# Forgetting attention: the product of weights and values with the values stationary and split in two parts

## The chip, the cores and the metric

The kernel runs on one core of one Trainium2 chip. The metric is device time in microseconds (us); lower is better. TensorE (PE) multiplies matrices: it holds a stationary operand, moves a second one past it, and writes sums to PSUM. VectorE (DVE), ScalarE (ACT) and GpSimd (POOL) work elementwise; SyncE (SP) issues the transfers. Each engine takes its instructions in a fixed order.

## The reference, cut to what matters

The program is a chain of two transformer blocks on 1024 tokens of width 1024. The change lies in the second block, in one of its three mixers, an attention with 8 heads of width 64 over 1040 tokens (16 meta tokens and 1024 others), causal, with a forgetting bias `c` (a running sum of log-sigmoids):

```python
s = jnp.einsum('bhqd,bhkd->bhqk', qb, kh).astype(jnp.float32) + (cb[..., :, None] - c[..., None, :])
s = jnp.where(kpos[None, :] <= qpos[:, None], s, -jnp.inf)
p = jax.nn.softmax(s, axis=-1)
return jnp.einsum('bhqk,bhkd->bhqd', p.astype(vh.dtype), vh)
```

Beside it run a recurrent mixer (RWKV, in chunks of 128 tokens) and a gated linear recurrence. Their outputs go through an output projection and then a feed-forward network with a gate.

## The kernel before, in words

One program holds all stages; a scheduler in the language orders the instructions of each engine at build time by a simulated timeline, with what is written first taken first. So parts that don't depend on each other are interleaved: `block2` (L1536) writes RWKV's chunks (L1553), then the projections of the attention (`fox_proj`, L1555), then `fox_att` (L1565); on the chip the attention fills the gaps of RWKV's last chunks, whose last operation on the output rows is L1302.

`fox_att` (L1442) loops over 8 heads. For each it loads the raw queries and keys (`fraw`, L1464, SyncE's queue) and splits each into a high part rounded to the type fp32r and a low rest (L1471 to L1477: ScalarE, VectorE, GpSimd; the query's and key's rows 64 to 127 carry rests and the bias). For an even head it loads the values of two heads (L1479 to L1481). Query tiles are 9: one of 16 rows, eight of 128 (`TILES`, L1364). `pipe` (L551) keeps two generators going, so that the first half of one tile's work is written next to the second half of the one before.

`fox_tile` (L1489) does one query tile `i`. First half: per chunk of up to 512 keys two fp32r products and a mask product into PSUM (L1506 to L1509), evacuation with a row maximum on VectorE (`evac_max`, L397), the negated maximum (L1514 to L1517), the exponential with its row sum on ScalarE (L1519), and the reciprocal (L1521). Second half: `wT` (L399) turns the weights, one transpose for each key tile (L405), with one copy from PSUM by ScalarE for up to four of them (L407); then, for each key tile, a plain fp32 product with the turned weights stationary and 64 columns of values moving (L1531), which the profile shows as two records; then the scaling by the reciprocal (L1532). In the odd head of a pair the tile's output rows are stored (L1534, SyncE's queue).

After the last head `done` frees RWKV's memory and loads the output weights, cast by ScalarE (L103) with the rest on VectorE (L106) in `wout_load` (L685). `out_proj2` (L1568) follows, one 128-row tile after another.

Of the PSUM banks (512 columns each) the attention uses two for scores (`sc`), two for transposes (`te`), one for the sums of the value products (`po`).

## Time and profile before

| | |
|---|---|
| Median of 3 runs | 3175.73 us (3175.03 to 3179.65) |
| Profiled execution, its own time | 3179.39 us |
| Span of the profile | 3177.6 us, 52057 instructions |
| TensorE busy | 3058.7 us (96%) |
| TensorE weight load busy | 2780.7 us (88%) |
| VectorE busy | 1863.2 us (59%) |
| ScalarE busy | 1401.9 us (44%) |
| GpSimd busy | 467.1 us (15%) |

The span runs from the first to the last instruction of the profiled execution. A busy TensorE is modelled, as its instructions overlap: the distance between starts says more than a duration. PEclk is the granted clock as a share of 2.4 GHz; the two levels are 1.2 and 2.4 GHz, so 0.59 means mostly the lower one. A row with a count covers that many instructions. "[1.86 <-DVE fo L1532]" behind a row is idle time of the engine before it and what ended it. The attention's first head starts at 2035 us of the span and the last one ends at 2305 us.

### The profile page before, as it was taken

Reading aid. Unit: us, or ns where it says so; the run is one execution under the profiler, and the core shown is the slowest. Engines: PE = TensorE matmul, PEld = TensorE weight load, DVE = VectorE, ACT = ScalarE, POOL = GpSimd, SP = SyncE. Lnnn points to the kernel's source line nnn. Section 1 sums busy time; section 2 is a strip of 40 time slices with the busy share of each in tenths; the row PEclk is TensorE's granted clock in tenths of the full one; section 3 lists DMA queues with packets and bytes.
Section 4 is the critical chain, followed back from the end, with each engine's and each line's share of the span. In section 5 each row is a group of like instructions: output and inputs, shape, how many; then the busy total and the mean of one; then the engine's idle time right before and its main releaser. Section 6 shows DMA issues by size and latency. Waiting matters only on the chain.

```text
span 3177.6 us, 52057 instructions
## 1 busy us (share of the span) xinstructions
PE 3058.7 (96%) x19891; PEld 2780.7 (88%) x19891; DVE 1863.2 (59%) x4889; ACT 1401.9 (44%) x3415; POOL 467.1 (15%) x506
## 2 busy tenths in 40 slices
PE   8899999999999999998999999999999999999997
PEld 5799999889878789997889999788879999999996
DVE  5777757677766665446547434666555344454446
ACT  4679845555553643323236121445534433233323
POOL 2467622331220000000000000201000000000003
PEclk9999999999999999999999899898999999999999
DMA  5222210110043221113321121313132111111113
GB/s 212 71 74 89 85 40 6 32 33 7 15 138 107 100 101 57 57 39 101 126 67 49 58 69 46 90 41 97 34 123 94 49 40 47 47 47 57 44 41 116
DMA packets 140330, 218.22 MB, mean 69 GB/s; under 512 B 24408, under 2 KB 80784, under 8 KB 140080
## 3 DMA queue, kind: packets, MB, share of 16 engines
q1 hardware_dynamic: 140080, 214.90, 21.5%
q8 instruction: 156, 2.56, 0.3%
q14 instruction: 94, 0.77, 0.1%
HBM read 171.87 MB, written 42.97 MB: 68 GB/s over the span
## 4 chain that ended last, share of the span: by engine, by line
PE 80%; DVE 7%; ACT 5%; DMA 3%; issue 2%; POOL 1%; SPq 0%; DVEq 0%; POOLq 0%; ACTq 0%
PE mm L132 17%; PE mm L133 16%; PE mm L134 16%; PE po L1531 3%; PE te L405 3%; PE sc L134 2%; PE sc L132 2%; PE sc L133 2%; PE sc L391 2%; PE po L661 2%; PE po L611 1%; DMA woraw<-in_w_out 1%; ACT EB L646 1%; ACT EA L596 1%; PE mm L149 1%
## 5 line engine op out<-in xcount | busy, mean ns | idle before, releaser
L132 PE MATMUL mm<-whi,hT 128*128 128x256 f32 (+1 forms) x1760 | 513.4, 292 | 15.3 <-DVE gs L428 3.4
L133 PE MATMUL mm<-wlo,hT 128*128 128x256 f32 (+1 forms) x1760 | 508.3, 289 | 3.9 <-POOL wlo L106 3.8
L132 PEld LDWEIGHTS mm<-whi,hT 128*128 128x128 f32 x1760 | 337.6, 192 | 24.1 <-ACT v L549 4.6
L133 PEld LDWEIGHTS mm<-wlo,hT 128*128 128x128 f32 x1760 | 337.7, 192 | 8.0 <-POOL wlo L106 5.1
L132 PE MATMUL mm<-hT3h,whi 128*128 128x342 f32 (+3 forms) x1020 | 325.9, 320 | 0.0
L133 PE MATMUL mm<-hT3l,whi 128*128 128x342 f32 (+3 forms) x1020 | 325.2, 319 | 0.0
L134 PE MATMUL mm<-hT3h,wlo 128*128 128x342 f32 (+3 forms) x1020 | 324.7, 318 | 0.0
L134 PE MATMUL mm<-whi,lo 128*128 128x256 f32 x1040 | 300.0, 289 | 2.5 <-POOL lo L106 2.4
L103 ACT CAST whi<-wraw 128x512 fp32r<-128x512 f32 (+2 forms) x205 | 136.0, 678 | 211.2 <-PE mm L133 85.0
L132 PE MATMUL mm<-hT,whi 128*128 128x352 f32 (+3 forms) x640 | 219.8, 344 | 2.9 <-ACT a L1018 1.8
L1659 DVE TENSOR_TENSOR acc<-acc,sc 128x512 f32<-128x512 f32 x160 | 108.8, 686 | 193.6 <-PE sc L134 192.8
L407 ACT COPY wT<-te 128x512 f32<-128x512 f32 (+2 forms) x368 | 160.5, 454 | 136.3 <-PE te L405 133.5
L133 PE MATMUL mm<-hT,whi 128*128 128x352 f32 (+3 forms) x640 | 218.7, 342 | 0.1
L134 PE MATMUL mm<-hT,wlo 128*128 128x352 f32 (+3 forms) x640 | 218.5, 343 | 0.0
L106 DVE TENSOR_TENSOR wlo<-wraw,whi 128x512 fp32r<-128x512 f32 (+1 forms) x161 | 126.0, 790 | 152.2 <-ACT whi L103 151.5
L134 PE MATMUL mm<-whi,hT 128*128 128x256 f32 (+3 forms) x720 | 205.8, 286 | 0.0
L134 PEld LDWEIGHTS mm<-whi,lo 128*128 128x128 f32 x1040 | 201.0, 193 | 5.2 <-POOL lo L106 3.3
L133 PEld LDWEIGHTS mm<-hT3l,whi 128*128 128x128 f32 x1020 | 192.0, 188 | 6.3
L132 PEld LDWEIGHTS mm<-hT3h,whi 128*128 128x128 f32 x1020 | 191.8, 188 | 6.0
L134 PEld LDWEIGHTS mm<-hT3h,wlo 128*128 128x128 f32 x1020 | 191.9, 188 | 3.6
L97 POOL TENSOR_TENSOR inv<-inv,cm 128x1 f32<-128x1 f32 (+1 forms) x87 | 53.2, 611 | 889.1 <-DVE inv L95 889.1
L97 POOL TENSOR_TENSOR c<-c,cm 128x2 f32<-128x2 f32 (+1 forms) x170 | 124.4, 733 | 384.5 <-DVE c L95 346.0
(491 smaller groups left out, 7740.8 us busy)
## 6 DMA issues: line engine op xcount, KB each, us to landing
adraw<-in_adaln_w SPq DMA_DIRECT2D x48, 512.0 KB, 3.8
wraw<-in_ffn_up SPq DMA_DIRECT2D x85, 256.0 KB, 2.8
wraw<-in_w_ab SPq DMA_DIRECT2D x26, 512.0 KB, 3.9
woraw<-in_w_out SPq DMA_DIRECT2D x48, 256.0 KB, 3.0
wraw<-in_w_gla SPq DMA_DIRECT2D x48, 256.0 KB, 2.8
wraw<-in_w_in SPq DMA_DIRECT2D x24, 512.0 KB, 4.3
dnraw<-in_ffn_down SPq DMA_DIRECT2D x44, 256.0 KB, 2.6
fraw<-qkd SPq DMA_DIRECT2D x32, 260.0 KB, 4.1
```

Source lines behind the costliest of these rows:

```text
L97: nc.gpsimd.tensor_tensor(out, out, self.cm05[:p, :n], op=ALU.pow)
L103: nc.scalar.copy(hi, src)
L106: (lo_eng or nc.vector).tensor_tensor(lo, src, hi.bitcast(F32), op=ALU.subtract)
L132: mmul(ps, ah, bh, start=k == 0, stop=False)
L133: mmul(ps, ah, bl, start=False, stop=False)
L134: mmul(ps, al, bh, start=False, stop=k == nk - 1)
L391: self.nc.tensor.matmul(sp, q[x][:, m], keys, start=x == 0, stop=last and x == 1)
L405: nc.tensor.transpose(ps[:n, j * 128:j * 128 + nq], E, self.ident[:nq, :nq])
L407: nc.scalar.copy(w[:n, :m, :nq], ps.rearrange("p (j t) -> p j t", j=4)[:n, :m, :nq])
L661: nc.tensor.matmul(ops[:, :128], w[:, x, :], v[:, i], start=x0 + x == 0, stop=x0 + x == len(kt) - 1)
L1531: nc.tensor.matmul(ops[:n, :64], w[:kn, y, :n], v[:kn, x, r], start=x == 0, stop=x == i)
L1659: nc.vector.tensor_tensor(acc[:, t, sl], acc[:, t, sl], ps, op=ALU.add)
```

## The change

Values become the stationary operand. For each head the values are split into an fp32r high part and a low rest that lie side by side (`vs`, 128 columns). Query tiles are handled in three groups, (0 to 3), (4 to 6) and (7, 8), by the new function `fox_tiles`. For each key tile `x` the weights of all query tiles of the group that see it are turned into one bank (up to 400 columns), copied to SBUF by ScalarE, rounded to fp32r (`hi`: ScalarE for even `x`, GpSimd for odd), and the rest taken by GpSimd (`lo`); two fp32r products, `hi` and `lo`, move past the same stationary values and add up over key tiles in one bank. The sums then lie with 64 + 64 value rows on partitions and query rows on columns; they are copied, turned back by one transpose for each query tile, and the two halves added and scaled. The evacuation of scores takes the negated scores and their minimum, which saves the separate negation. Buffers for a prepared head go from three to two, the value buffer from two to one, and the exponentials' buffers from four of one tile to two of one group. The output rows are stored at the end of a group. Where the removed lines only repeat the function printed above they are cut.

```diff
--- before.py
+++ after.py
@@ -1447,7 +1447,7 @@
         s0 = p.tile([128, 8], F32, name="foxsel0", bufs=1)
         nc.sync.dma_start(s0, I["fox_sel"])
         nc.vector.tensor_copy(sel, s0)
-        kcs = [p.tile([128, T], F32R, name=f"fkc{i}", bufs=1) for i in range(3)]
+        kcs = [p.tile([128, T], F32R, name=f"fkc{i}", bufs=1) for i in range(2)]
         cn = p.tile([128, T], F32, tag="fraw", name="cn")
         nc.sync.dma_start(cn[64:128], cnd)
         for kc in kcs:
@@ -1464,10 +1464,10 @@
                         nc.sync.dma_start(raw[64 * e:64 * e + 64], qkd[pr, part, r])
                     raws.append(raw)
 
-                qh = p.tile([128, T], F32R, tag="fqh", name="fqh", bufs=3)
-                ql = p.tile([128, T], F32R, tag="fql", name="fql", bufs=3)
-                kh = p.tile([128, T], F32R, tag="fkh", name="fkh", bufs=3)
-                kc = kcs[h % 3]
+                qh = p.tile([128, T], F32R, tag="fqh", name="fqh")
+                ql = p.tile([128, T], F32R, tag="fql", name="fql")
+                kh = p.tile([128, T], F32R, tag="fkh", name="fkh")
+                kc = kcs[h % 2]
                 nc.scalar.activation(qh, raws[0], AF.Copy, scale=0.125)
                 nc.vector.scalar_tensor_tensor(ql[0:64], raws[0][0:64], 0.125, qh[0:64].bitcast(F32), op0=ALU.mult,
                                                op1=ALU.subtract)
@@ -1476,62 +1476,100 @@
                 nc.gpsimd.tensor_copy(kc[0:64], kh[0:64])
                 nc.vector.tensor_tensor(kh[64:128], raws[1][64:128], kh[64:128].bitcast(F32), op=ALU.subtract)
                 if m == 0:
-                    v = p.tile([128, 9, 128], F32, tag="fv", name="fv")
+                    v = p.tile([128, 9, 128], F32, tag="fv", name="fv", bufs=1)
                     nc.sync.dma_start(v[:16, 0], vd[0:16, pr * 128:pr * 128 + 128])
                     nc.sync.dma_start(v[:, 1:9], vd[16:1040, pr * 128:pr * 128 + 128].rearrange("(t p) d -> p t d", p=128))
                     o = p.tile([128, 9, 128], F32, tag="fo", name="fo", bufs=1)
-                for i in range(9):
-                    yield self.fox_tile(pr, m, i, qh, ql, kh, kc, v, o, o2d)
+
+                vs = p.tile([128, 9, 2, 64], F32R, tag="fvs", name="fvs")
+                for z in ((slice(0, 128), slice(1, 9)), (slice(0, 16), slice(0, 1))):
+                    nc.scalar.copy(vs[z][:, :, 0], v[z][:, :, r])
+                    nc.gpsimd.tensor_tensor(vs[z][:, :, 1], v[z][:, :, r], vs[z][:, :, 0].bitcast(F32), op=ALU.subtract)
+                for tiles in ((0, 1, 2, 3), (4, 5, 6), (7, 8)):
+                    yield self.fox_tiles(pr, m, tiles, qh, ql, kh, kc, vs, o, o2d)
             done()
 
         self.pipe(heads())
 
-    def fox_tile(self, pr, m, i, qh, ql, kh, kc, v, o, o2d):
+    def fox_tiles(self, pr, m, tiles, qh, ql, kh, kc, vs, o, o2d):
 
         nc, p = self.nc, self.ap_
-        T = 1040
         r = slice(64 * m, 64 * m + 64)
-        c0, n = self.TILES[i]
-        nk = c0 + n
-        if i == 0:
-            cks = [(0, 16)]
-        else:
-            cks = [(0, min(nk, 400))] + [(a, min(512, nk - a)) for a in range(400, nk, 512)]
...
+        ends = [c0 + n for c0, n in self.TILES]
+        E_ = p.tile([128, 1968], F32, tag="fE", name="fE")
+        l, nM = self.small(4, "fl"), self.small(4, "fnM")
+        Es, cols, a, c = [], [], 0, 0
+        for y, i in enumerate(tiles):
+            c0, n = self.TILES[i]
+            nk = ends[i]
+            E = E_[:, a:a + nk]
+            Es.append(E)
+            cols.append(slice(c, c + n))
+            a, c = a + nk, c + n
+            cks = [(0, min(nk, 400))] + [(x, min(512, nk - x)) for x in range(400, nk, 512)]
+
+            mx = nM[:, y:y + 1] if len(cks) == 1 else self.small(4, "fmx")
+            for ci, (k0, kn) in enumerate(cks):
+                sp = self.sc()
+                ks = slice(k0, k0 + kn)
+                last = ci == len(cks) - 1
+                nc.tensor.matmul(sp[:n, :kn], qh[:, c0:c0 + n], kh[:, ks], start=True, stop=False)
+                nc.tensor.matmul(sp[:n, :kn], ql[:, c0:c0 + n], kc[:, ks], start=False, stop=not last)
+                if last:
+                    nc.tensor.matmul(sp[:n, kn - n:kn], self.ident_r[:n, :n], self.masks_r[:n, 2, :n],
+                                     start=False, stop=True)
+                nc.vector.tensor_scalar(E[:n, ks], sp[:n, :kn], -1.0, None, op0=ALU.mult, op1=ALU.min,
+                                        accum_out=mx[:n, ci:ci + 1])
+            if len(cks) > 1:
+                nc.vector.tensor_reduce(nM[:n, y:y + 1], mx[:n, :len(cks)], axis=AX.X, op=ALU.min)
+            nc.scalar.activation(E[:n], E[:n], AF.Exp, bias=nM[:n, y:y + 1], scale=-1.0, accum_out=l[:n, y:y + 1])
+        rl = self.small(4, "frl")
+        small = 1 if tiles[0] == 0 else 0
+        if small:
+            nc.vector.reciprocal(rl[:16, :1], l[:16, :1])
+        nc.vector.reciprocal(rl[:, small:len(tiles)], l[:, small:len(tiles)])
         yield
+
         ops = self.po()
-        steps = [(self.wT([E[:n, 0:16]], n), 0, 0)]
-        for x0 in range(1, i + 1, 4):
-            grp = range(x0, min(x0 + 4, i + 1))
-            w = self.wT([E[:n, self.TILES[x][0]:self.TILES[x][0] + 128] for x in grp], n)
-            steps += [(w, y, x) for y, x in enumerate(grp)]
-        for w, y, x in steps:
-            kn = self.TILES[x][1]
-            nc.tensor.matmul(ops[:n, :64], w[:kn, y, :n], v[:kn, x, r], start=x == 0, stop=x == i)
-        nc.vector.tensor_scalar(o[:n, i, r], ops[:n, :64], rl[:n], None, op0=ALU.mult)
+        for x in range(tiles[-1] + 1):
+            ys = [y for y, i in enumerate(tiles) if i >= x]
+            k0, kn = self.TILES[x]
+            ps = self.te()
+            for y in ys:
+                n = cols[y].stop - cols[y].start
+                nc.tensor.transpose(ps[:kn, cols[y]], Es[y][:n, k0:k0 + kn], self.ident[:n, :n])
+            z = slice(0, kn), slice(cols[ys[0]].start, c)
+            et = p.tile([128, 400], F32, tag="fet", name="fet")
+            nc.scalar.copy(et[z], ps[z])
+            hi = p.tile([128, 400], F32R, tag="feh", name="feh")
+            lo = p.tile([128, 400], F32R, tag="fel", name="fel")
+            if x % 2:
+                nc.gpsimd.tensor_copy(hi[z], et[z])
+            else:
+                nc.scalar.copy(hi[z], et[z])
+            nc.gpsimd.tensor_tensor(lo[z], et[z], hi[z].bitcast(F32), op=ALU.subtract)
+            w = vs[:kn, x].rearrange("p e d -> p (e d)")
+            for e, h in enumerate((hi, lo)):
+                nc.tensor.matmul(ops[:, z[1]], w, h[z], start=x + e == 0, stop=e == 1 and x == tiles[-1],
+                                 skip_group_check=True)
+        ot = p.tile([128, 400], F32, tag="fot", name="fot")
+        nc.scalar.copy(ot[:, :c], ops[:, :c])
+        ps = self.te().rearrange("p (y e d) -> p y e d", y=4, e=2)
+        for y in range(len(tiles)):
+            n = cols[y].stop - cols[y].start
+            nc.tensor.transpose(ps[:n, y].rearrange("p e d -> p (e d)"), ot[:, cols[y]], self.ident)
+        t = p.tile([128, 4, 64], F32, tag="ft", name="ft")
+        parts = [(slice(0, 128), slice(small, len(tiles)))] + [(slice(0, 16), slice(0, 1))] * small
+        for rows, ys in parts:
+            nc.scalar.copy(t[rows, ys], ps[rows, ys, 1])
+            nc.vector.tensor_tensor(t[rows, ys], t[rows, ys], ps[rows, ys, 0], op=ALU.add)
+            shape = [rows.stop, ys.stop - ys.start, 64]
+            nc.vector.tensor_tensor(o[rows, tiles[0] + ys.start:tiles[0] + ys.stop, r], t[rows, ys],
+                                    rl[rows, ys].unsqueeze(2).to_broadcast(shape), op=ALU.mult)
         if m == 1:
-            nc.sync.dma_start(o2d[i][:, pr * 128:pr * 128 + 128], o[:n, i])
+            for i in tiles:
+                n = self.TILES[i][1]
+                nc.sync.dma_start(o2d[i][:, pr * 128:pr * 128 + 128], o[:n, i])
 
     def block2(self, close_hT, w2, first, o2d, lod):
```

## Rows read from the trace of the kernel before

**Rows 1.** Windows: length, busy (xcount) of PE, PEld, DVE, ACT, POOL; granted clock, DMA share, GB/s.

```profile
2035.00:2182.00 147.00, 146.76 (x1099) 127.79 (x1097) 105.99 (x400) 72.41 (x181) 17.77 (x19) 1.00 0.18 44
2182.00:2200.00 18.00, 16.14 (x77) 14.88 (x76) 8.43 (x25) 8.28 (x22) 1.74 (x1) 0.59 0.74 198
2236.00:2306.00 70.00, 69.53 (x523) 60.79 (x523) 34.67 (x174) 40.74 (x113) 0.00 (x0) 1.00 0.08 22
```

**Rows 2.** PE's timeline: head starts 0, 3, 5, 7, and the last value products; start, length.

```profile
2035.13 0.39 PE L405 MATMUL te<-ident_r,fE 16*16 16x16 f32 x2
2166.36 0.18 PE L405 MATMUL te<-ident_r,fE 16*16 16x16 f32 x1
2235.51 0.18 PE L405 MATMUL te<-ident_r,fE 16*16 16x16 f32 x1
2281.97 0.18 PE L405 MATMUL te<-ident_r,fE 16*16 16x16 f32 x1
2304.22 1.10 PE L1531 MATMUL po<-fv,wT 128*128 128x64 f32 x8
```

**Rows 3.** PE's timeline in head 7: start, length, instruction, count.

```profile
2299.36 1.58 PE L1531 MATMUL po<-fv,wT 16*128 16x64 f32 x10
2300.78 0.27 PE L405 MATMUL te<-ident_r,fE 128*16 128x128 f32 x1
2300.88 0.78 PE L1531 MATMUL po<-fv,wT 128*128 128x64 f32 x6
2301.50 1.04 PE L405 MATMUL te<-ident_r,fE 128*128 128x128 f32 x8
2302.47 1.47 PE L1531 MATMUL po<-fv,wT 16*128 16x64 f32 x10
```

**Rows 4.** Chain of waits between 2182 and 2236 us: start, length, what.

```profile
2183.32 1.98 DVE fkh L1477
2221.60 3.04 DMA woraw<-in_w_out
```

**Rows 5.** PE's timeline in head 6: two score pairs, 400 and 512 columns.

```profile
2266.22 0.43 PE L1506 MATMUL sc<-fkh,fqh 128*128 128x400 f32 x1
2266.48 0.34 PE L1507 MATMUL sc<-fkc,fql 128*128 128x400 f32 x1
2266.66 0.39 PE L1506 MATMUL sc<-fkh,fqh 128*128 128x512 f32 x1
2266.89 0.39 PE L1507 MATMUL sc<-fkc,fql 128*128 128x512 f32 x1
```

**Rows 6.** Groups of instructions, 2020 to 2306 us, ScalarE: count, busy us, mean ns, idle before.

```profile
L407 ACT COPY wT<-te 128x512 f32<-128x512 f32 x48 | 27.6, 583 | 28.5 <-PE te L405 28.1 <-PE po L1531 0.3
L407 ACT COPY wT<-te 128x256 f32<-128x256 f32 x16 | 5.9, 369 | 6.5 <-PE te L405 6.5
L103 ACT CAST wo<-woraw 128x512 fp32r<-128x512 f32 x16 | 9.8, 612 | 7.9 <-DMA woraw<-in_w_out 7.9
L1475 ACT CAST fkh<-fraw 128x1040 fp32r<-128x1040 f32 x8 | 8.4, 1052 | 10.1 <-DMA fraw<-qkd 9.9
```

**Rows 7.** Groups of instructions: GpSimd in the whole run, VectorE in 2020 to 2306 us.

```profile
L182 POOL TENSOR_TENSOR adacc<-adacc,adpr 128x512 f32<-128x512 f32 x84 | 108.7, 1296 | 40.2 <-ACT adpr L179 27.3 <-ACT adacc L179 7.3 <-PE sc L391 3.2
L182 POOL TENSOR_TENSOR adacc<-adacc,adpr 128x256 f32<-128x256 f32 x28 | 20.7, 739 | 13.8 <-ACT adpr L179 6.6 <-ACT adacc L179 5.8
L1474 POOL CAST fql<-foxsel 64x1040 fp32r<-64x1040 f32 x8 | 8.6, 1081 | 63.7 <-PE sc L1507 52.6 <-PE sc L1509 9.7 <-DVE foxsel L1449 1.3
...
L106 DVE TENSOR_TENSOR wo<-woraw,wo 128x512 fp32r<-128x512 f32 x16 | 11.5, 717 | 9.2 <-ACT wo L103 9.1
```

**Rows 8.** Timeline of SyncE's queue, 2174 to 2180 us.

```profile
2174.90 5.69 SPq L1534 DMA_DIRECT2D o<-fo  x3
```

**Rows 9.** GpSimd's timeline: the same cast alone, and beside VectorE.

```profile
2102.66 1.05 POOL L1476 CAST fkc<-fkh 64x1040 fp32r<-64x1040 f32 x1 [0.90 <-ACT fkh L1475]
2182.47 1.74 POOL L1476 CAST fkc<-fkh 64x1040 fp32r<-64x1040 f32 x1 [0.96 <-ACT fkh L1475]
```

More of the change, by code (lines that the diff above doesn't have):

```diff
@@ L1485, in heads @@
+                for tiles in ((0, 1, 2, 3), (4, 5, 6), (7, 8)):
+                    yield self.fox_tiles(pr, m, tiles, qh, ql, kh, kc, vs, o, o2d)
             done()
         self.pipe(heads())
-    def fox_tile(self, pr, m, i, qh, ql, kh, kc, v, o, o2d):
+    def fox_tiles(self, pr, m, tiles, qh, ql, kh, kc, vs, o, o2d):
         nc, p = self.nc, self.ap_
-        T = 1040
         r = slice(64 * m, 64 * m + 64)
-        c0, n = self.TILES[i]
-        nk = c0 + n
-        if i == 0:
-            cks = [(0, 16)]
-        else:
-            cks = [(0, min(nk, 400))] + [(a, min(512, nk - a)) for a in range(400, nk, 512)]
-        E = p.tile([128, T], F32, tag="fE", name="fE", bufs=4)
-        mx = self.small(4, "fmx")
-        for ci, (k0, kn) in enumerate(cks):
-            sp = self.sc()
-            ks = slice(k0, k0 + kn)
-            last = ci == len(cks) - 1
-            nc.tensor.matmul(sp[:n, :kn], qh[:, c0:c0 + n], kh[:, ks], start=True, stop=False)
-            nc.tensor.matmul(sp[:n, :kn], ql[:, c0:c0 + n], kc[:, ks], start=False, stop=not last)
-            if last:
-                nc.tensor.matmul(sp[:n, kn - n:kn], self.ident_r[:n, :n], self.masks_r[:n, 2, :n],
-                                 start=False, stop=True)
-            self.evac_max(E[:n, ks], sp[:n, :kn], mx[:n, ci:ci + 1])
-        nM = self.small(1, "fnM")
-        if len(cks) > 1:
-            nc.vector.tensor_reduce(nM[:n], mx[:n, :len(cks)], axis=AX.X, op=ALU.max)
-            nc.vector.tensor_scalar(nM[:n], nM[:n], -1.0, None, op0=ALU.mult)
-        else:
-            nc.vector.tensor_scalar(nM[:n], mx[:n, :1], -1.0, None, op0=ALU.mult)
-        l = self.small(1, "fl")
-        nc.scalar.activation(E[:n, :nk], E[:n, :nk], AF.Exp, bias=nM[:n], accum_out=l[:n])
-        rl = self.small(1, "frl")
-        nc.vector.reciprocal(rl[:n], l[:n])
```

## The prediction, made before the changed kernel was run

> **What bounds the kernel now.** First the windows view of the stretch in which the changed code runs [rows 1]. From 2035 to 2182 us TensorE is busy 146.76 of 147 us: it shares that stretch with the RWKV chunks, whose instructions stand earlier in the program. From 2236 to 2306 attention is nearly alone, and TensorE is busy 69.53 of 70 us, ScalarE 40.74, VectorE 34.67, GpSimd not at all. Busy matmuls are modelled and could hide slack, so I read the distance between head starts next: the 16x16 transpose of tile 0 marks one per head [rows 2]. Heads 0 to 2 took (2166.36 - 2035.13)/3 = 43.7 us each beside RWKV; heads 5 and 6 took (2281.97 - 2235.51)/2 = 23.2 us alone. Then the starts of consecutive matmuls in the last head [rows 3]: 16 value products' records in 1.42 + 0.62 us, 0.128 us apart, and 9 transposes in 0.10 + 0.97 us, 0.119 apart, with nothing between. TensorE is packed: TensorE's issue sets the pace of both stretches.
>
> The 3.35 heads done by 2182 (146.9 us / 43.7 with head 3 beginning at 2166.36) used 3.35 x 23.2 = 77.7 us of TensorE; RWKV had the other 69. After 2182 there are 4.65 heads in 2305.3 - 2182 = 123 us, which is 107.9 us at 23.2 and 15.4 us lost. The loss is visible: the granted clock in 2182 to 2200 is 0.59, mostly the lower level of 1.2 GHz, after TensorE waited for VectorE to prepare head 4 [rows 1, 4], and later a wait of 3.04 us for an output weight, behind which the queues of ScalarE and VectorE stood [rows 4].
>
> **The change, part by part, per head.**
>
> *TensorE.* Removed: 45 plain fp32 value products, two records each: 90 x 0.128 = 11.5 us. Added: for key tile x one high and one low product over all query tiles of the group that see it. The groups have 4, 7 and 9 key tiles, so 40 products; their columns are 400+384+256+128 = 1168, 5x384+256+128 = 2304 and 8x256+128 = 2176, together 5648, moved twice: 11296. The score products are of this single-pass type: 400 columns took 0.18 us to the next start, 512 took 0.23 [rows 5], so 0.45 ns a column: 5.1 us, plus 0.4 us because the six 128-column ones cannot go below the 0.12 us of a short product, plus 20 times the 0.08 us by which a first product behind a short one took longer (0.26 against 0.18) [rows 5]: 7.1 us. Transposes stay 45 and become 54 with the sums turned back: 9 x 0.119 = 1.1 us. So 23.2 - 11.5 + 7.1 + 1.1 = 19.9 us a head, 3.3 us less.
>
> *ScalarE.* It is busy 40.74/70 x 23.2 = 13.5 us a head now, plus 2 x 1.05 us of preparation, which that window lacks [rows 1, 6]. The copies of transposed weights stay the same in columns: 128x512 takes 583 ns and 128x256 takes 369, so 0.155 us + 0.836 ns a column; 20 copies of 5648 columns are 7.8 us, against the 9 + 12 copies they replace, about the same. New: casting the high part for even x, 11 casts of 3088 columns, at 612 ns for 512 and 1052 for 1040 [rows 6], so 0.185 + 0.833 ns a column: 4.6 us; values' high part 0.85; three copies of the sums, 1040 columns, 1.3; four small copies 1.1. Total 13.5 + 2.1 + 7.9 = 23.5 us.
>
> *GpSimd.* It is nearly idle now. New: 20 subtractions of 5648 columns. The nearest rows are two-input operations in the first layer: 1296 ns for 512 columns, 739 for 256 [rows 7], so 0.18 us + 2.18 ns a column: 15.9 us. The high part for odd x, 2560 columns at the 1081/1040 ns of a cast [rows 7]: 2.7. Values' low part, 512 and 64 columns: 1.6. The two casts it has already: 2.1 or more. Total 22.3 us, so GpSimd goes from the emptiest engine to above TensorE's 19.9. The row for the same subtraction on VectorE, 717 ns for 512 columns [rows 7], says that GpSimd takes 1.8 times as long. The Trainium skill, "GPSIMD Engine Reference", section "Engine selection", speaks against the change here: for elementwise work on two inputs it sends the reader to VectorE, GpSimd being about twice as slow. By that rule the low parts on VectorE would be near half of the GpSimd sum, an estimate; the trace agrees in the ratio of 1.8.
>
> *VectorE.* The evacuation takes a minimum of the negated scores at the same size, nine negations and five reciprocals go, and nine scalings of a tile by the inverse sum become four additions and four products. From 34.67 of 70 us busy it stays far from the bound [rows 1]: nothing.
>
> *Queues and buffers.* The 36 stores of the output move from each tile to the end of a group; one batch already held SyncE's queue for 5.69 us [rows 8], and the loads of the next head's keys stand behind them. A head of over 20 us covers this; uncovered, it is up to 5.7 us in each of four odd heads, 23 us in all. Preparing one head ahead instead of two and one value buffer instead of two are covered in the same way. The one constant copy less at the start is hidden by the loads that it stands beside.
>
> **What a head costs once RWKV is done.** From below: the largest engine sum, 23.5 (ScalarE) or 22.3 (GpSimd); TensorE alone would allow 19.9. From above: one step goes transpose, copy 0.48, cast 0.50, subtraction 1.02 (384 columns), product, and two buffers let two steps overlap: (2.0 + 0.3 of handing over)/2 = 1.15 us a step, plus up to half of a 1.0 us exponential that stands ahead on ScalarE: 1.4 to 1.65, with 20 narrower and wider steps about 28, with GpSimd's preparation about 31. I take 26, nearer the lower end, because ScalarE and GpSimd overlap and neither is full.
>
> **The sum.** Until 2182 the 77.7 us of TensorE hold 77.7/19.9 = 3.90 heads where they held 3.35. I take 0.8 of that gain, 3.79, as each engine's order is fixed in advance. Of the 4.21 heads left, at 26 us: 109.5 us. Of the 15.4 us lost now I keep half, 8, since TensorE has slack to catch up with. In the last head's 6 us of slack the next stage (L1568) can start with the tiles already stored: -5. Output-weight casts on a fuller ScalarE: +1. So 113.5 us against 123: **9.5 us less**. On the profiled execution, 3179.39 us (span 3177.6, the rest before and after it), this gives 3169.9; that execution is 3.7 us above the median of 3175.73, so on the median **3166 us**.
>
> **The rivals.**
>
> *GpSimd's chain is the new bound (slower).* Its casts and VectorE's operations get in each other's way: the 64x1040 cast took 1.05 us alone, and 1.74 where VectorE worked beside it, and VectorE's subtraction then took 1.98 [rows 4, 9]. Now GpSimd would be busy most of the time, through RWKV's part too. At the upper end of 31 us a head: 4.21 x 31 + 4 = 134.5, so +11.5: 3187 us. It decides from (123 - 4)/4.21 = 28.3 us a head. For it: the two-deep buffers. Against: the evacuation reads PSUM and is most of VectorE's work here. The Trainium skill, "SBUF — State Buffer", section "SBUF: two separate sides", makes it a rule: GpSimd and VectorE share a pair of ports that is locked for a whole instruction, against a VectorE operation with two SBUF inputs. By that rule, the trace agrees in the 1.74 and 1.98 us.
>
> *The full relief (faster).* ScalarE and GpSimd stay under TensorE's old 23.2 us and only TensorE counts: 3.3 us x 8 heads would be 26 at the most; with the 23.5 of ScalarE after 2182: 4.1 x 23.5 + 4 = 100, 23 us less: 3153 us.
>
> *Nothing moves.* RWKV's order and waits, not TensorE's load, set how many heads are done by 2182; then 4.65 x 26 + 4 = 125, +2: 3178 us. TensorE's 100% in that stretch speaks against it.
>
> *The clock falls.* Waits between short products leave TensorE idle, and the clock goes to 1.2 GHz as at 2182 [rows 1]. Two of the four heads at 2 x 19.9 = 39.8 us: 2 x 39.8 + 2.2 x 26 + 4 = 141, +18: 3194 us. Against: TensorE would still have 20 of 26 us of work, in short pieces, where the fall at 2182 came after one long gap; I hold this for the least likely.
>
> That the products are not single-pass I exclude: the score products of the same type run at 0.18 us for 400 columns [rows 5].
>
> **How the numbers follow.** About 0.2% (6 us) is what a measurement of this kernel can tell from no change. Chances: forecast 0.34, full relief 0.16, nothing moves 0.20, GpSimd's chain 0.20, clock 0.10. The forecast has a part inside 6 us, about 0.06, and GpSimd's chain one below +6 us, nearly 0; the nothing case one above, about 0.04. Faster: 0.28 + 0.16 = 0.44; same: 0.16 + 0.06 = 0.22; slower: 0.34. The range reaches from the lower end of full relief to the clock's case, 3148 to 3196; the forecast's own, from 24.5 to 27.5 us a head, is 3160 to 3172.
>
> **What would show it.** Value products: 40 records a head where 90 were, about 0.18 us apart at 400 columns. The distance of head starts: near 38 to 40 us beside RWKV (43.7 now), 24.5 to 27.5 alone (23.2 now). GpSimd near 22 us busy a head with subtractions near 1.0 us for 384 columns; ScalarE near 23. If GpSimd's subtractions are well above 1.05 us or TensorE waits for them most, the chain is the bound; if starts alone are below 24, the full relief. RWKV ending (L1302) later than 2182 would break the sum, as would a granted clock below 0.9 from 2200 on.

## The result, and the profile after

The changed kernel takes 3252.73 us in the median (3249.19 to 3255.45, 4 runs) against 3175.89 us for the kernel before beside it: ratio 1.0239, 95% interval [1.0221, 1.0257], 77 us slower, where 9.5 us less was forecast. The profiled execution has a span of 3247.4 us. Everything lies in the attention's stretch: its last products end near 2372 us of the span, before at 2305 [rows 2].

The page of the changed kernel, busy time of each engine: TensorE and ScalarE have gained 25 and 57 us, GpSimd 169, VectorE nothing.

```profile
PE 3083.3 (95%) x19563; PEld 2774.5 (85%) x19563; DVE 1863.2 (57%) x4769; ACT 1458.6 (45%) x3566; POOL 636.4 (20%) x754
```

Windows of the changed kernel (length, busy of PE, PEld, DVE, ACT, POOL, granted clock, DMA share, GB/s), to be read beside [rows 1]:

```profile
2035.00:2100.00 65.00, 62.98 (x434) 53.51 (x434) 49.01 (x154) 32.93 (x86) 29.41 (x41) 0.97 0.09 22
2100.00:2150.00 50.00, 45.31 (x276) 37.18 (x274) 34.92 (x98) 27.46 (x70) 25.70 (x34) 0.91 0.29 79
2150.00:2200.00 50.00, 34.24 (x148) 23.29 (x149) 23.53 (x66) 30.82 (x74) 24.72 (x33) 0.75 0.36 101
2200.00:2250.00 50.00, 38.97 (x174) 28.05 (x173) 21.70 (x67) 32.39 (x79) 32.39 (x43) 0.73 0.23 59
2250.00:2300.00 50.00, 41.23 (x183) 30.21 (x181) 16.83 (x63) 31.40 (x83) 31.28 (x43) 0.72 0.04 10
2300.00:2350.00 50.00, 42.61 (x215) 31.17 (x215) 18.66 (x80) 35.52 (x93) 31.80 (x50) 0.89 0.03 8
```

From 2150 on no engine is full, and the granted clock is between 0.72 and 0.89 where the kernel before had 1.00 in its heads 5 to 7. From 2150 to 2300 that is a good half of the time at 1.2 GHz. The starts of heads 0, 1, 2, 3, 5 and 7 on TensorE and its last value product, as in [rows 2], then the last operation of RWKV on VectorE:

```profile
2030.64 0.18 PE L1540 MATMUL te<-ident_r,fE 16*16 16x16 f32 x1
2097.54 0.61 PE L1540 MATMUL te<-ident_r,fE 16*16 16x16 f32 x4
2151.95 0.60 PE L1540 MATMUL te<-ident_r,fE 16*16 16x16 f32 x4
2201.28 0.60 PE L1540 MATMUL te<-ident_r,fE 16*16 16x16 f32 x4
2275.22 0.61 PE L1540 MATMUL te<-ident_r,fE 16*16 16x16 f32 x4
2341.24 0.60 PE L1540 MATMUL te<-ident_r,fE 16*16 16x16 f32 x4
2371.84 0.33 PE L1553 MATMUL po<-fel,fvs 128*128 128x128 f32 x1
2138.99 0.50 DVE L1302 SCALAR_TENSOR_TENSOR o<-bn,o 128x256 f32<-128x256 f32 x1
```

Two things are to be seen. RWKV ends at 2139, 42 us earlier than before (2180.7): TensorE is 97% busy until 2100 and what the attention leaves free goes to RWKV, whose instructions stand earlier. Heads 0 and 1 take 66.9 and 54.4 us beside it, where 38 to 40 were forecast. So only 1 + (2139.0 - 2097.5)/54.4 = 1.76 heads are done by then. The other 6.24 heads take 2371.8 - 2139.0 = 232.8 us, **37.3 us a head**, where 26 were forecast. Heads 6 and 7, with no later head to prepare, take 30.4 and 30.9.

Groups of the changed kernel between 2025 and 2380 us (count, busy, mean ns of one, idle before):

```profile
L1550 POOL TENSOR_TENSOR fel<-fet,feh 128x256 fp32r<-128x256 f32 x72 | 52.8, 743 | 18.1 <-PE po L1553 10.5 <-ACT fet L1543 2.5 <-ACT feh L1549 2.3
L1550 POOL TENSOR_TENSOR fel<-fet,feh 128x384 fp32r<-128x384 f32 x40 | 40.1, 1012 | 18.0 <-PE po L1553 11.3 <-ACT fet L1543 2.5 <-PE te L1540 2.3
L1543 ACT COPY fet<-te 128x256 f32<-128x256 f32 x72 | 26.6, 369 | 26.6 <-POOL fel L1550 21.5 <-PE te L1540 4.3
L1521 DVE TENSOR_SCALAR_CACHE_REDUCE fE<-sc 128x400 f32<-128x400 f32 x48 | 27.4, 571 | 39.6 <-PE te L1540 35.5 <-PE sc L1517 2.1 <-PE sc L1519 1.5
```

The single operations cost what [rows 6, 7] said (739 ns and 369 ns for 256 columns). What is new is the waiting around them. One such place, in head 4: TensorE's timeline, and below it the same microseconds on ScalarE, VectorE and GpSimd.

```profile
2244.90 0.52 PE L1553 MATMUL po<-fel,fvs 128*128 128x256 f32 x1
2247.78 0.48 PE L1553 MATMUL po<-feh,fvs 128*128 128x128 f32 x1 [2.36 <-POOL feh L1547]
2249.37 1.02 PE L1560 MATMUL te<-ident_r,fot 128*16 128x128 f32 x4 [0.58 <-ACT fot L1556]
2251.65 1.54 PE L1540 MATMUL te<-ident_r,fE 128*128 128x128 f32 x6 [0.61 <-ACT fet L1543]
2243.19 1.05 ACT L1471 ACTIVATE fqh<-fraw 128x1040 fp32r<-128x1040 f32 x1
2244.15 1.04 ACT L1475 CAST fkh<-fraw 128x1040 fp32r<-128x1040 f32 x1
2245.60 1.98 DVE L1477 TENSOR_TENSOR fkh<-fraw,fkh 64x1040 fp32r<-64x1040 f32 x1
2245.25 1.23 POOL L1476 CAST fkc<-fkh 64x1040 fp32r<-64x1040 f32 x1 [1.04 <-ACT fkh L1475]
2246.43 1.29 POOL L1547 CAST feh<-fet 128x128 fp32r<-128x128 f32 x1
```

The preparation of a later head stands in the queues of ScalarE, GpSimd and VectorE between two steps. The last 128 columns of the group wait for GpSimd behind it, and their cast takes 1.29 us beside VectorE's subtraction (the same cast of 256 columns takes 0.41 us on average). Then the end of the group follows, a copy and four transposes, and TensorE waits again. Behind it six transposes take 1.54 us, 0.26 each where 0.119 was the distance before [rows 3]: the granted clock is 0.50 from 2245 to 2257.

### The profile page after: what moved, and what is told of

Same layout as the page of the kernel before. It is cut to its first block, busy times and chain, and to the rows that moved or that the text cites. A ratio compares the mean times of both kernels' runs of the same rounds, so it can differ in the third digit from the quotient of the medians.

```text
span 3247.4 us, 51910 instructions
## 1 busy us (share of the span) xinstructions
PE 3083.3 (95%) x19563; PEld 2774.5 (85%) x19563; DVE 1863.2 (57%) x4769; ACT 1458.6 (45%) x3566; POOL 636.4 (20%) x754
## 4 chain that ended last, share of the span: by engine, by line
PE 78%; DVE 8%; ACT 5%; DMA 4%; issue 3%; POOL 2%; SPq 0%; POOLq 0%; DVEq 0%; ACTq 0%
PE mm L132 16%; PE mm L133 16%; PE mm L134 16%; PE sc L391 2%; PE sc L134 2%; PE sc L132 2%; PE sc L133 2%; PE po L661 2%; PE po L1553 2%; PE te L1540 2%; PE te L405 2%; DMA woraw<-in_w_out 1%; PE po L611 1%; ACT EB L646 1%; PE tp L255 1%
## 5 line engine op out<-in xcount | busy, mean ns | idle before, releaser
L1677 ACT COPY fx<-mm 128x342 f32<-128x342 f32 (+2 forms) x132 | 58.5, 444 | 230.7 <-PE mm L134 229.4
```

## The experiments

All ratios are to the kernel before, measured beside each run; a difference of 0.0010 is 3.2 us. Each edit also has the scheduler order the instructions anew, so what an edit gives holds the effect of another order too; no run parts the two. The theories: **GpSimd** (the low parts hold the steps), **buffers**, **banks** of PSUM, **preparation** and **output weights** (work of other heads or stages queued between the steps), **clock** (the low clock itself is the cost). The "steps" of the expectations are the chain from transpose to product for each key tile.

### GpSimd's low part

```diff
-            nc.gpsimd.tensor_tensor(lo[z], et[z], hi[z].bitcast(F32), op=ALU.subtract)
+            nc.vector.tensor_tensor(lo[z], et[z], hi[z].bitcast(F32), op=ALU.subtract)
```

> The low part of the turned weights is taken by VectorE where GpSimd took it; the values' low part stays on GpSimd. Theory 'GpSimd': the low parts are what a step waits for; on VectorE a 128x256 one takes about 0.4 us where GpSimd took 0.743, so with 20 steps a head, two of them overlapping, 3 to 7 us a head and, for the five heads after RWKV, 15 to 35 us come back: 3218 to 3238 us. Theory 'clock' (a chain of small waits leaves TensorE idle, the granted clock falls to 0.72 and its work takes longer): the shorter step gives a part back and the clock of 2200 to 2300 rises above 0.80; the time is in the same range, so the two part on the clock: by 'GpSimd' it can stay near 0.72. Theory 'buffers' (the two-deep rings and the two buffers of exponentials): within 6 us of the changed kernel, 3247 to 3259.

Measured: 3226.20 us, 1.0139 [1.0123, 1.0156], 32 us less than the changed kernel, by the difference of the ratios. Heads 3 to 6 fall from 36.6, 37.4, 35.7 and 30.4 us to 32.3, 34.1, 34.1 and 28.6. The group of low parts, same stretch:

```profile
L1550 DVE TENSOR_TENSOR fel<-fet,feh 128x256 fp32r<-128x256 f32 x72 | 29.4, 422 | 11.3 <-POOL feh L1547 9.7 <-PE po L1553 1.2 <-ACT feh L1549 0.3
```

422 ns for 743. The granted clock of 2200 to 2300 went from 0.73 to 0.80, at the line that the clock theory had drawn, so this run does not part the two. That the low parts on GpSimd are on the path is shown; that they are all is refuted, as 44 us are left.

### Deeper rings, more buffers for the exponentials

```diff
-            et = p.tile([128, 400], F32, tag="fet", name="fet")
+            et = p.tile([128, 400], F32, tag="fet", name="fet", bufs=4)
...
-        E_ = p.tile([128, 1968], F32, tag="fE", name="fE")
+        E_ = p.tile([128, 1968], F32, tag="fE", name="fE", bufs=3)
```

The first line (with `feh` and `fel` alike) is one run, the second another.

> The copy of the turned weights, their high and their low part get four buffers each in place of two. Theory 'buffers, of the steps': with four steps in flight TensorE's transposes run ahead, the waits of ScalarE's copy for GpSimd's low part (22 us from 2180 to 2380) go, and a head after RWKV comes to 26 us or less: at least 30 us less, 3220 or below. Theory 'buffers, of the exponentials': TensorE waits at the group's border all the same; -10 to 0. Theory 'GpSimd': GpSimd is 63% busy from 2200 to 2300, so it has room: -20 to 0 us. Theory 'clock' says nothing of its own but that any gain comes with a higher granted clock.

> Three buffers for a group's exponentials in place of two. In the changed kernel VectorE waited 58 us from 2180 to 2380 for TensorE's transposes before it could empty scores of a later group. Theory 'buffers, of the exponentials': these waits hold up the scores, TensorE has nothing at the group's border: 15 to 40 us less, 3213 to 3238. Theory 'steps' or 'preparation': the wait is VectorE's spare time; within 6 us of 3253.

Measured: rings of four 3245.36 us, 1.0208 [1.0184, 1.0233]; three buffers of exponentials 3271.01 us, 1.0284 [1.0261, 1.0307]. Rings give some 10 us at the edge of the intervals where 30 were expected, so they are not what holds the steps. More exponentials made it slower by some 14 us, which no theory expected: heads 3 to 6 took 38.9, 40.1, 39.1 and 35.8 us. VectorE's wait for a buffer, 58 us from 2180 to 2380, stayed with the third one (56 us) and was not what held the steps; why the run is slower is open.

### The split straight from PSUM

```diff
-            et = p.tile([128, 400], F32, tag="fet", name="fet")
-            nc.scalar.copy(et[z], ps[z])
...
-            if x % 2:
-                nc.gpsimd.tensor_copy(hi[z], et[z])
-            else:
-                nc.scalar.copy(hi[z], et[z])
-            nc.gpsimd.tensor_tensor(lo[z], et[z], hi[z].bitcast(F32), op=ALU.subtract)
+            nc.scalar.copy(hi[z], ps[z])
+            nc.vector.tensor_tensor(lo[z], ps[z], hi[z].bitcast(F32), op=ALU.subtract)
```

> The copy of the turned weights to SBUF is left out: ScalarE rounds the high part straight from PSUM, VectorE subtracts it from PSUM to give the low part. A step then goes transpose, ScalarE, VectorE, product: two handovers of about 1.0 us together where there were three of 2.0. ScalarE loses 7.8 us a head, GpSimd 18.6. Theory 'GpSimd' and theory 'clock' both: a head after RWKV falls to 20 to 25 us, near TensorE's own sum of 19.9: 40 to 70 us less than the changed kernel, 3183 to 3213; by 'clock' with a granted clock above 0.9 in that stretch. Theory 'buffers, of the exponentials': the wait at the group's border stays, and VectorE, which empties the scores too, is busier: -20 to 0, 3233 to 3253.

Measured: 3229.26 us, 1.0154 [1.0133, 1.0175]: 27 us less, half of what was expected. A step is one operation and its handover shorter, and heads 3 to 6 still take 37.1, 32.3, 33.5 and 31.8 us. So the step's own length was not the main thing left.

### The banks

```diff
             for h in range(8):
+                if h == 3:
+                    self.psum(te="DA", po="CE")
```

> The split from PSUM, and from head 3 on four PSUM banks for turned weights in place of two and two for the sums of the value products in place of one, RWKV's banks being free by then. Theory 'banks' (at the group's border the first product of the next group waits until the sums are copied, and transposes wait for the high and low parts to be read): 15 us or more below the split alone, 3214 or less. Theory 'preparation': the idle time comes from the queues of ScalarE and VectorE, not from the banks: within 8 us of 3229.

> The changed kernel, and from head 3 on four PSUM banks for turned weights and two for the sums of the value products; copy, casts and GpSimd's low parts stay. With the split from PSUM the banks gave 26 us. Theory 'banks': the group's border is a wait of its own, and they give 15 to 30 us here too: 3223 to 3238. Theory 'GpSimd': behind the copy to SBUF the banks come free early anyway and GpSimd's chain of 0.74 to 1.0 us a low part holds the pace: within 8 us of 3253.

Measured: with the split 3202.72 us, 1.0067 [1.0048, 1.0086], 28 us less than the split alone. Heads 4 to 6 come to 26.8, 27.3 and 24.2 us, and head 7 to 22.3 at a granted clock of 1.00. On the changed kernel, with its copy and GpSimd's parts, 3241.59 us, 1.0206 [1.0189, 1.0223], 10 us less, between the two expectations and at the edge of the intervals. The banks pay more where the steps are short. Starts of transposes in the last head of the run with both, TensorE's timeline:

```profile
2321.23 0.38 PE L1542 MATMUL te<-ident_r,fE 128*128 128x128 f32 x2
...
2321.81 0.38 PE L1542 MATMUL te<-ident_r,fE 128*128 128x128 f32 x2
...
2322.41 0.38 PE L1542 MATMUL te<-ident_r,fE 128*128 128x128 f32 x2
```

0.58 and 0.60 us for a step of two transposes and two products of 256 columns. The prediction's terms give 0.24 + 0.23 + 0.08 = 0.55: TensorE's term for a step was right where it doesn't wait.

### The preparation

```diff
-                nc.scalar.activation(qh, raws[0], AF.Copy, scale=0.125)
+                nc.gpsimd.tensor_scalar(qh, raws[0], 0.125, None, op0=ALU.mult)
...
-                nc.scalar.copy(kh, raws[1])
+                nc.gpsimd.tensor_copy(kh, raws[1])
...
-                nc.vector.tensor_tensor(kh[64:128], raws[1][64:128], kh[64:128].bitcast(F32), op=ALU.subtract)
+                nc.gpsimd.tensor_tensor(kh[64:128], raws[1][64:128], kh[64:128].bitcast(F32), op=ALU.subtract)
```

This edit was put on the split, on split and banks, and on the kernel before; one run leaves the preparation of heads 4 to 7 out of the changed kernel.

> Heads 4 to 7 are not prepared: their queries and keys are not loaded and split, they use the split tiles of heads 2 and 3 (so the output of heads 4 to 7 is not the reference's). Everything else stays. In the changed kernel the preparation of the head after next stands in the queues of ScalarE (1.05 + 1.04 us), VectorE (1.23 + 1.98) and GpSimd (1.05 + 1.23) between two steps, in the alone stretch TensorE then idles up to 2.4 us at a time and its granted clock is 0.50 for some 10 us. Theory 'preparation': heads 2 to 5 fall from 36 to 37 us to the 30.4 of the heads without one, four times 6 us: 20 to 30 us less than the changed kernel, 3223 to 3233, and the clock of 2200 to 2300 rises. Theory 'steps' (the chain over ScalarE and GpSimd alone sets the pace): what the engines do between steps costs its own 2 to 3 us at most, 4 x 2.5: 3243 or above.

> The high and low parts straight from PSUM by ScalarE and VectorE, and the whole preparation of a head's queries and keys on GpSimd but for the low part of the queries. Beside the split from PSUM alone (3229 us), in which ScalarE's 1.07 us and VectorE's 1.98 us of preparation stand between the steps and TensorE's clock is 0.50 to 0.61 right behind: theory 'preparation': a head after RWKV falls from 32 to 37 us by 4 to 6, so 20 to 30 us less than that, 3200 to 3210. Theory 'steps': within 8 us of 3229.

> The split from PSUM, the banks, and the preparation on GpSimd but for the queries' low part. From 3203 us: heads 3 to 5 (33.8, 26.8, 27.3 us) lose their 4 us of preparation on ScalarE and VectorE: theory 'preparation' 8 to 14 us less, 3189 to 3195. If GpSimd's preparation gets in VectorE's way instead, 3203 or more. By neither is it below the kernel before: TensorE's own work a head is about 21 us and RWKV's stretch holds fewer heads.

> The kernel before, with the preparation of queries and keys on GpSimd but for the queries' low part. There heads 3 and 4 took 33.8 and 35.3 us where heads 5 and 6, with no preparation beside them, took 23.3 and 23.1, and TensorE's clock fell to 0.59 behind a wait for VectorE's low part of the keys (1.98 us). Theory 'preparation' (queued work of 2 to 3 us on ScalarE and VectorE is what lets the clock fall): 5 to 12 us less than before, ratio 0.996 to 0.998. Rival (the key's loads, or the end of RWKV, made those heads long): ratio within 0.001 of 1, or above where GpSimd, slower on two inputs, is late.

Measured: left out 3240.18 us, 1.0184 [1.0159, 1.0209], 17 us less than the changed kernel, short of the 20 to 30 expected; on the split 3224.51 us, 1.0140 [1.0115, 1.0164]; on split and banks 3199.01 us, 1.0074 [1.0057, 1.0092]; on the kernel before 3182.06 us, 1.0009 [0.9994, 1.0023]. The last three are no different from the kernels that they were put on. Leaving the work out helps, moving it alone does not. Either another thing fills the same queues, or GpSimd is late with what was moved to it; the next edits look at the first.

### The output weights

Waits of the changed kernel between 2139 and 2240 us (total, times, longest):

```profile
DVE wo L106 <- ACT wo L103: 15.4, 9, 5.0
ACT wo L103 <- DMA woraw<-in_w_out: 12.9, 10, 5.5
PEld te L1560 <- ACT fot L1556: 9.1, 5, 6.2
```

ScalarE waits up to 5.5 us for a load of the next stage's weights, with the copy of the attention's sums behind it in its queue, and TensorE waits up to 6.2 us for that copy (until 2171.4 us, with the granted clock at 0.50 from 2168 to 2176). The kernel before has 7.9 us of ScalarE's wait [rows 6]. Edits: three raw buffers, or the splitting on GpSimd:

```diff
-                wo.append(self.wout_load(wos.enter_context(self.pool("wo2", 1)), self.I["w_out2"]))
+                wo.append(self.wout_load(wos.enter_context(self.pool("wo2", 1)), self.I["w_out2"], raws=3))
```

```diff
+                if aside == 1:
+                    nc.gpsimd.tensor_copy(h[:, 0][sl], raw)
+                    nc.gpsimd.tensor_tensor(h[:, 1][sl], raw, h[:, 0][sl].bitcast(F32), op=ALU.subtract)
+                    continue
...
-                wo.append(self.wout_load(wos.enter_context(self.pool("wo2", 1)), self.I["w_out2"]))
+                wo.append(self.wout_load(wos.enter_context(self.pool("wo2", 1)), self.I["w_out2"], aside=1))
```

> The changed kernel with three raw buffers in place of two for the output weights, so that a load is issued one split earlier. In the changed kernel ScalarE waited 12.9 us from 2139 to 2240 for these loads, 5.5 at a time, with copies of the sums and weights queued behind. Theory 'output weights': these waits shrink by half or more and 5 to 12 us come back: 3241 to 3248. Rival (the waits fall where the steps wait anyway): within 4 us of 3253.

> The split from PSUM and the banks (3203 us), and the output weights split on GpSimd, so that no wait for their loads stands in ScalarE's queue and no 0.69 us subtraction in VectorE's between the steps. Theory 'output weights': 10 to 20 us less, 3183 to 3193. Rival: GpSimd's 16 x (0.6 + 1.3) us get in the way of VectorE's low parts, or the wait was covered: 3198 to 3208.

> The kernel before with the output weights split on GpSimd. There the chain from 2182 to 2236 holds a wait of 3.04 us for a load, and ScalarE waited 7.9 us in all for these loads. Theory 'output weights': 4 to 9 us less, ratio 0.997 to 0.9985. Rival (TensorE is packed, and what heads 3 and 4 lose comes from the preparation): ratio within 0.001 of 1.

Measured: three buffers 3250.51 us, 1.0218 [1.0198, 1.0239], not told apart from the changed kernel; on split and banks 3202.70 us, 1.0056 [1.0037, 1.0075], 3 us less, a miss (nine of its ten executions lie between 3189 and 3208 us); on the kernel before **3171.50 us, 0.9977 [0.9962, 0.9992]**, as expected, and faster than both kernels. In that run head 4 fell from 35.3 to 27.8 us. The windows of 2200 to 2236 (columns as in [rows 1]), first the kernel before, then the run:

```profile
2200.00:2236.00 36.00, 33.17 (x192) 26.73 (x192) 24.01 (x79) 23.69 (x57) 2.96 (x2) 0.78 0.34 106
```

```profile
2200.00:2236.00 36.00, 35.20 (x244) 30.15 (x244) 22.69 (x100) 22.69 (x58) 15.65 (x15) 0.94 0.22 73
```

### All causes together

> The split from PSUM, the banks from head 3 on, and on GpSimd both the preparation (but for the queries' low part) and the splitting of the output weights. By the theory that these are the causes, the alone heads come to 24 to 27 us and the sum is the kernel before within 12 us: 3180 to 3192 (3178 before). Rival: GpSimd, which now waits for the output weights' loads with the preparation queued behind them, is late with heads 4 and 5: 3195 or more.

> As the run before, with the four banks for turned weights and the two for sums from head 2 on, so that head 2 has them as soon as RWKV's last products are read. Theory 'banks': head 2 falls from 35 to 30 us, 3 to 6 us less than the run before. Rival (head 2 is slow because RWKV's last operations and the first loads stand beside it, and the banks are RWKV's until then): the same within 3 us, or slower where the first step of head 2 waits for RWKV's banks.

Measured: split, banks, preparation and output weights 3181.74 us, 1.0001 [0.9982, 1.0021]; with the banks from head 2 on (`h == 2` above) 3175.50 us, 0.9986 [0.9960, 1.0012]. The first hits its forecast: **the 77 us are gone, within some 6 us either way.** One of the four edits, that of the output weights, also made the kernel before faster (0.9977); against that kernel 1.0001 - 0.9977, 8 us, would be left, which the intervals don't tell from nothing. The six heads from 2 on take (2309.9 - 2153.2)/6 = 26.1 us each. The two runs are not told apart, and head 2, whose fall the second was to show, is at 27.2 us in the first already. Starts of heads 2 to 5 in the first of them:

```profile
2153.17 0.60 PE L1546 MATMUL te<-ident_r,fE 16*16 16x16 f32 x4
2180.32 0.60 PE L1546 MATMUL te<-ident_r,fE 16*16 16x16 f32 x4
2206.00 0.60 PE L1546 MATMUL te<-ident_r,fE 16*16 16x16 f32 x4
2235.37 0.61 PE L1546 MATMUL te<-ident_r,fE 16*16 16x16 f32 x4
```

Heads 2 and 3 took 27.2 and 25.7 us. With split and banks alone they took 38.4 and 33.8, with the preparation moved 37.8 and 33.1, with the output weights moved 34.7 and 36.0. Each of the two edits is worth nothing measurable, both together 1.0067 - 1.0001, 21 us: this fits that either work in those queues is enough to hold the steps. The profiles show it less sharply: the attention ends at 2326 us with split and banks, at 2318 and 2313 with one edit more, and at 2310 with both. The profiled execution with the output weights moved, 3189.22 us, is the shortest of its run, and in the one with both, head 2 starts 15 us later.

### The clock by itself

One product a step, or four, of two constants, were added from about head 3 on (`k` = 1 or 4); a third run added three products tied to the step's own high part, on the kernel with rings of four:

```diff
+            for _ in range(k):
+                nc.tensor.matmul(self.fill[:, :384], self.ident_r, self.masks_r.rearrange("p a b -> p (a b)"), start=True, stop=True)
...
+            for _ in range(3):
+                nc.tensor.matmul(self.fill[:, z[1]], w, hi[z], start=True, stop=True, skip_group_check=True)
```

> From head 3 on each step issues one more product, behind the transposes and ahead of the value products: two constants, 384 columns, into a bank of its own that nothing reads. Five heads of 20 steps at 0.17 us (0.45 ns a column at 2.4 GHz) add 17 us to TensorE's work, at 1.2 GHz 34. Theory 'clock': the added product keeps TensorE busy in the waits, the granted clock of 2200 to 2350 goes from 0.72 to above 0.9, and the time falls by 5 to 40 us though more is computed: 3213 to 3248. Rival, the clock is only a sign of the waits and the path is the chain over ScalarE and GpSimd: the time stays within 6 us where the product hides in the waits, or rises by up to 34: 3247 to 3287.

> As the run with one added product a step, with four of them: from head 3 on, 20 steps x 4 products of 384 columns, 13.6 us a head at 2.4 GHz and 27 at 1.2, in place of 3.4 and 6.8. TensorE then has 33 to 36 us of work a head at 2.4 GHz and hardly an idle time left. Theory 'clock': it stays at the upper level (granted clock above 0.95 from 2220 on) and a head takes 34 to 37 us, what it takes in the changed kernel without the added work (36): within 12 us of the changed kernel, 3241 to 3265. Rival, the waits of the chain are the path and the clock follows from them without mattering: most of the added work falls outside the waits, 8 to 14 us a head or more: 3293 to 3330.

> The changed kernel with rings of four (3245 us), and from head 3 on, behind the two value products of a step, three more with the same high part and the same values into a bank that nothing reads; they can't start before the step's own products, so they stay in the steps. They add 3 x 5648 columns, 7.6 us a head at 2.4 GHz (15 at 1.2), 38 or 76 us in five heads. Theory 'clock' (the low clock itself is what makes a head long): TensorE is busy where it waited, the granted clock of 2200 to 2350 rises from 0.78 above 0.9, and what comes back pays for most of the added work: 3245 to 3258. Rival, waits: the clock may rise, but the waits on ScalarE and GpSimd remain and the added work, in the queue ahead of the next transposes, falls partly on the path: 3260 to 3300.

Measured: one 3265.91 us, 1.0266 [1.0244, 1.0289]; four 3298.19 us, 1.0381 [1.0365, 1.0397]; tied 3272.20 us, 1.0292 [1.0264, 1.0319]. The first two say nothing of the theory: the order of TensorE's instructions, fixed at build time, pulled the constant products together ahead of the steps. Windows of the added products alone in the run with four (length, PE, PEld, clock, DMA share, GB/s):

```profile
2150.00:2200.00 50.00, 43.21 (x212) 35.34 (x211) 1.00 0.40 123
2200.00:2250.00 50.00, 34.85 (x170) 28.48 (x168) 1.00 0.04 9
2250.00:2300.00 50.00, 0.00 (x0) 0.00 (x0) 0.76 0.25 65
```

Where they ran the clock was 1.00, and 0.76 as soon as they were over. The tied ones stayed in the steps (from 2200 on 74 to 78 records in each 50 us); the clock of 2200 to 2300 rose from 0.78 to 0.86, over heads 3 to 7 from 0.79 to 0.86, and heads 3 to 5 became longer, not shorter: 37.1, 38.0 and 40.2 us for 34.5, 34.3 and 34.2. Of some 40 us of added work at 2.4 GHz, 1.0292 - 1.0208 = 27 us showed in the time. That falls in the rival's range (3260 to 3300). But over these heads the clock stayed below the 0.9 that the test asked for, so the run speaks against the clock as the whole cost and does not settle its share: no run changes the clock alone.

What the share could be, as an estimate: along the chain of waits from 2180 to 2380 in the changed kernel TensorE's five lines have 22.8 + 21.0 + 6.8 + 4.6 + 4.0 = 59%, 118 us. The granted clock of these 200 us is 0.76, so 48% of the time is at half speed, which makes 118 x 0.48 / 2 = 28 us. The whole stretch from 2139 to 2372 can be read the same way. TensorE is idle for 48 of the 233 us and busy for 185 at a clock of 0.75, where 6.24 heads at the prediction's 19.9 us would be 124. Of the 61 us more of busy time the lower clock for half of the time would make up to 185 x 0.5 / 2 = 46. So by this estimate idle time and slower products are of like size. Both go with the waits: in the first run with all causes together TensorE is idle for 18 of the 155 us from 2155 to 2310, at a clock of 0.92.

## Why the prediction was wrong

**The durations held.** ScalarE's copies and GpSimd's subtractions came out as costed from [rows 6, 7], and TensorE's step, where it doesn't wait, as costed from [rows 3, 5]. GpSimd was busy 63.7 of the 100 us from 2200 to 2300 at 37 us a head, 23.6 us a head for 22.3 forecast. From 2140 to 2372 no engine waits for a load of queries, keys or values, so the later stores cost nothing there, as forecast.

**The count of heads failed, at the cost of the forecast gain.** "I take 0.8 of that gain, 3.79" heads by 2182: it was 2 + (2182 - 2152)/49.3 = 2.6. The heads took longer beside RWKV too, 66.9 and 54.4 us, and the time of TensorE that they left went to RWKV. But what RWKV takes early it doesn't take later: 6.24 heads at the forecast 26 us, and 4 of loss, from 2139 would end at 2305, the same as before. This step alone turns the 9.5 us of gain into no change.

**"I take 26" us a head is the step that failed**, and with it its upper end of 31. It was 37.3, (37.3 - 26) x 6.24 = 70 us. The upper end priced a step as copy, cast, subtraction and handing over, with two steps overlapping and half an exponential ahead on ScalarE. What other work stands in the same queues was counted as busy time of an engine that isn't full, so at next to nothing: the preparation "covered" by a head of over 20 us but for GpSimd's part, 3 us in the upper end; the output weights at +1; the wait at the end of a group with one bank not at all. The runs put the low parts on GpSimd at 32 us, the copy and GpSimd's parts of a step at 27, the preparation at 17 (left out), the banks at 10 to 28; they overlap. The split from PSUM, the banks, the moved preparation and the moved output weights together give back 76 of the 77 us. How much of a head is waiting and how much is products at the lower clock behind the waits stays open.

**Where the relief sits.** In the kernel before the value products waited for one copy by ScalarE, and a packed TensorE hid everybody's waits. The change took 3.3 us a head off TensorE, by the prediction's sum, and put two or three operations of ScalarE and GpSimd between a step's transposes and its products. With the four edits the time equals the kernel before: the relief itself gave nothing that could be measured, as heads 2 to 7 still take 23 to 29 us, 26.1 on average, where 23.2 was the packed pace. That average is the prediction's 26, by luck: these steps have no copy, and no low part on GpSimd.

**The rivals.** GpSimd's chain (3187, chance 0.20) was right in its mechanism, as one part: 32 us by the run on VectorE, and the 1.29 us cast beside VectorE's 1.98 is the row that it spoke of. (The cast that [rows 9] calls alone also had VectorE beside it, in L1472, which began 0.4 us after it and took 1.74 us for the 1.23 us at 2182.) The Trainium skill, "GPSIMD Engine Reference", section "Engine selection", sends such two-input work to VectorE; this case agrees, 743 ns against 422. The clock (3194, chance 0.10) was there in every alone head, where the argument that TensorE's work comes in short pieces, without one long gap, had held it for least likely. From 2200 on no wait of TensorE was longer than 2.5 us, and its clock was at 1.2 GHz for half of the time. But the clock came with the waits, and what part of the cost it is was not shown. The rivals were priced as if only one could come true, and both were priced too low: 11.5 + 18 us together are still far from 77. So the range ended at 3196, 57 us short.

## What to carry to other kernels

Before work is moved from a packed engine into a chain over several others, list what else stands in those engines' queues between two links of the chain: preparation of later items, loads of the next stage with their casts, the end of a group. Each can count with its full length, and with its load's wait, not with the engine's share of busy time; and taking one out may show nothing while another remains. In the kernel before the same reading paid: the next stage's weights, split on the nearly idle GpSimd, gave 0.23%.

## What was not expected of the hardware

In the run with split and banks the granted clock fell with TensorE shown as busy throughout. Windows of RWKV's end, columns as in [rows 1]:

```profile
2126.00:2133.00 7.00, 7.00 (x52) 6.02 (x51) 3.23 (x12) 3.19 (x10) 0.00 (x0) 1.00 0.02 4
2133.00:2140.00 7.00, 7.00 (x24) 4.71 (x24) 3.75 (x13) 1.53 (x4) 1.11 (x1) 0.64 0.10 26
2140.00:2147.00 7.00, 7.00 (x29) 6.25 (x28) 3.45 (x9) 1.08 (x3) 0.00 (x0) 0.50 0.00 1
```

Seven of seven microseconds busy in all three, at clocks of 1.00, 0.64 and 0.50, and half the instructions in the lower two. A full row of busy time does not say that the clock is at its upper level; whether the engine really had no gap there the modelled ends can't tell.
